# A transformer block on one core: the values of retention and attention made in one stage ahead of the heads, by seven half-size products

## The chip, the cores and the metric

The kernel runs on one core of one Trainium2 chip. The metric is the device time of one execution in microseconds (us), as the median of several runs. A core has five engines with a queue of instructions each: TensorE (PE in the profile; its weight loads are PEld), VectorE (DVE), ScalarE (ACT), GpSimd (POOL) and SyncE (SP). The instructions of one engine run in the order of its queue, and wait for others by semaphores. SyncE, ScalarE and GpSimd also issue transfers (DMAs) between the chip's DRAM and the on-chip buffers, in the same queues.

## The reference

One block works on 528 tokens (16 meta tokens and 512 real ones) of width 1024, in fp32: a feed-forward layer, a mixer, a second feed-forward layer and a last norm. The mixer has two branches that share one input projection.

```python
def hybrid_mixer(u, pos, k_top, w_in, w_ret_out, w_att_out, w_mix_out):
    proj = u @ w_in
    ...
    rq, rk, rv, rg, aq, ak, av, iq, ik, iw, g_ret, g_att = jnp.split(proj, offs, axis=-1)
    rq = rope(rq.reshape(B, T, RET_HEADS, RET_DK), pos)                      # 4 heads of 256
    rk = rope(rk.reshape(B, T, RET_HEADS, RET_DK), pos) * (RET_DK ** -0.5)
    rv = rv.reshape(B, T, RET_HEADS, RET_DV)                                 # 4 heads of 512
    yr = retention(rq.transpose(0, 2, 1, 3), rk.transpose(0, 2, 1, 3), rv.transpose(0, 2, 1, 3))
    ...
    yr = (jax.nn.silu(rg) * yr) @ w_ret_out
    aq, ak = rope(aq, pos), rope(ak, pos)                                    # 8 heads of 128
    iq, ik = rope(iq, pos), rope(ik, pos)                                    # 8 index heads of 64
    ya = dsa_attention(aq, ak, av, iq, ik, iw, k_top).reshape(B, T, ATT_W) @ w_att_out
    merged = jax.nn.sigmoid(g_ret) * yr + jax.nn.sigmoid(g_att) * ya
    return merged @ w_mix_out

def reference(...):
    h = h + 0.5 * swiglu(rmsnorm(h, ffn1_norm), ...)
    h = h + hybrid_mixer(rmsnorm(h, mix_norm), pos, k_top, ...)
    h = h + 0.5 * swiglu(rmsnorm(h, ffn2_norm), ...)
    return rmsnorm(h, final_norm)[:, N_META:]
```

The values are `rv` (2048 columns of the projection) and `av` (1024 columns). `retention` multiplies decayed query-key products by values; `dsa_attention` picks the 128 best keys of a query by the index scores and attends to them and to the meta tokens.

## The kernel before

**Products.** Activations lie transposed: width on the 128 partitions, tokens along the free axis, in eight tiles of 128 rows (`KD` = 8). An fp32 product is made of three products of parts: each operand is split into a high and a low part (`split`: ScalarE copies the high part, VectorE subtracts it for the low one), and TensorE makes high x high, low x high and high x low. `mm3` (L145) does this for a tile of 128 output columns: 8 x 3 = 24 matmuls of 128x512. Weights come from DRAM by SyncE in pieces of 512 KB or 1 MB (`load_w`, `raw`, two buffers) and are split in pieces of 128x1024 (`split_w`; `whi`, `wlo`, three buffers each). `Cols` hands out such pieces of a weight matrix, tile after tile.

**Feed-forward layers.** They use a Strassen-Winograd scheme (`Sevens`): a product in two halves on each side is made by seven half-size products in place of eight, of sums of tokens and sums of weights that VectorE makes. The steps are run by `steps_through` (L273), which interleaves by hand the split of the next weights with the matmuls of a step; there the orders of PE, ACT and DVE are written out. Elsewhere only PE's order is written out, and a scheduler orders the other engines' work.

**Mixer.** The tokens are not multiplied by their norm ahead of the projections. The factor of each token (`R`, a row over tokens copied to all partitions, or `rtok`, a column) is applied to what comes out: the rope tables are multiplied by it (`rope_tables`, L859, on GpSimd), gates are multiplied on VectorE (L1232, L1079 and `gate_a`, L1262), values are multiplied in `split_gain` (L120). The order of TensorE is:

1. Index queries (four psiq), head 0's keys (psrk), index keys (psik) and their ropes, in the pool `ixt`.
2. Four retention heads (the loop in the pool `rt`): projections of queries and keys (psrq, psrk) and the output products of the head before (`ret_out`, psro) alternate; then `values` (L1014) for this head, `decayed` (psst: key-query products and their decay, L1139), gates of the head (psrg), and the products with the values (`weigh`). Index scores (`index_steps`, pssc) and the top-k selection (`select_steps`) run in small steps in between, called by `step`.
3. Attention (the pool `ao`): keys and queries (psak, psaq) of a head, `scores`, transposes, products with values; the values of the first four heads are made ahead of head 0 (`half_values`), those of the last four in head 3. The gates of both branches stand between (`wide_gate`, `wide_gate_a`).
4. The output projections of both branches and the second feed-forward layer.

`values` makes 512 columns of values for the 512 tokens, tokens on the partitions: 96 matmuls (psv, L1037) of 128x512 on `w_in`, plus the 16 meta tokens by 32 small ones (psvl, L1049, two records each in the profile). High and low parts of the result (`vo`) stay on chip; the meta tokens' rows make a trip through DRAM (`vd`) to lie as tails under the others (`place_tails`). It is called six times: four retention heads, two halves of the attention.

Of the kernel before, what the change touches and what calls it, by code (L numbers as in the profile page):

```python
# [18 lines left out]
P = 128  # L19
# [16 lines left out]
IH = 8  # L36
# [45 lines left out]
def kernel(ctx: ExitStack, tc: tile.TileContext, x, meta, g1, wg1, wu1, wd1, gm,  # L82
# [73 lines left out]
    class Cols:  # L156
# [5 lines left out]

        def next(self):
# [34 lines left out]
    def tmp():  # L198
        return tp["pool"].tile([P, T], F32, tag="tmp", name="tmp", bufs=tp["bufs"])

    def rstd_steps(ssum, n, dim, dst, sp, psum, r=None):
# [7 lines left out]
        yield from rstd_of(col, n, dim, dst, sp, psum, P - (n - S), r)  # L209

    def rstd_of(col, n, dim, dst, sp, psum, tail, r=None):

# [4 lines left out]
        if r is None:  # L217
            r = sp.tile([P, 5], F32, tag="rcol", name="rcol", bufs=2)
# [35 lines left out]
    vd = dpool.tile([2, P, P], F32, name="vd")  # L254
# [5 lines left out]

    rtok = cpool.tile([P, 8], F32, name="rtok")
# [11 lines left out]
    def steps_through(steps):  # L273
# [8 lines left out]
        def upper(i):  # L282
            if i < len(steps):
                v = steps[i][1]()
                n, c = v.shape[1:]
                hi, lo = (wpool.tile([P, 1024 + WPAD], F32R, tag=t, name=t, bufs=3)[:, w_at[0] : w_at[0] + n * c]
# [223 lines left out]


    with pool("f1") as fp, ExitStack() as later:
# [7 lines left out]
        def mm_tile(name):  # L520
# [110 lines left out]
        with tc.manual_schedule(engines={mybir.EngineType.PE, mybir.EngineType.Activation, mybir.EngineType.DVE}):  # L631
            pss = [mm_tile("psg"), mm_tile("psg")]
# [73 lines left out]
        hidp = later.enter_context(pool("hid"))  # L706
        ttp = later.enter_context(pool("tt"))
        s1 = Sevens(T, TX, wg1, wu1)
# [12 lines left out]
        with tc.manual_schedule(engines=BUSY):  # L721
            psus = [mm_tile("psu")]
            mm3(halves(psus[0])[0], w0, xs, KD)
            psus.append(mm_tile("psu"))
            part = halves(psus[1])[0]
            mm3(part[:1], w1, xs, KD)
            psr = mm_tile("psr")
# [12 lines left out]
            pss = [mm_tile("psg")]  # L740
# [9 lines left out]
            pss.append(mm_tile("psg"))  # L750
# [7 lines left out]
            psus = [mm_tile("psu")]  # L758
# [6 lines left out]
            psus.append(mm_tile("psu"))  # L765
# [32 lines left out]
        def leave_tokens(k):  # L798

            h, l = new_x(k, XO)  # L800
            nc.gpsimd.tensor_scalar(xlast[:, k, :NM], hT[k][:, S:], gains[:, 1, k : k + 1], None, ALU.mult)
# [12 lines left out]
        steps += down(groups[-1], 6, leave_tokens)  # L814
        pipe = steps_through(steps)
        with tc.manual_schedule(engines=BUSY):
# [13 lines left out]
            s1.banks = later.enter_context(pool("f1banks", 8, PSUM))  # L830
# [19 lines left out]
        wss.close()  # L850
        sqp.append(later.enter_context(pool("sq", 1, side="right")))
        for _ in pipe:
            pass
    R = R2
    Rr = R[:, REAL]
# [3 lines left out]
    def rope_tables(i, mp):  # L859
# [4 lines left out]
        nc.gpsimd.tensor_tensor(c, c, R, ALU.mult)  # L864
        nc.gpsimd.tensor_tensor(s, s, R, ALU.mult)
        return c, s

    mixps = ExitStack()
    mmp = mixps.enter_context(pool("mxmm", 2, PSUM))
    smp = mixps.enter_context(pool("mxsm", 4, PSUM))  # L870

    def sm_tile(name):
        return smp.tile([P, S], F32, tag="sm", name=name)

    def mm_tile(name):
        return mmp.tile([P, 1024], F32, tag="mm", name=name)
# [40 lines left out]
    with pool("ixt") as ixt:  # L917
        tp.update(pool=ixt, bufs=8)
        norm = rstd_steps(ssum2, T, D, R2, ixt, lambda: mm_tile("psn"), rtok)
        pss = []  # L920
        cols = Cols(w_in, OFF_IQ, 4)
        for i in range(4):
            w = cols.next()
            ps = sm_tile("psiq")[:, :NL]
            mm3([(ps, LATE)], w, xs, KD)
            pss.append(ps)
            if i < 3:
                next(norm)
        nc.gpsimd.tensor_tensor(xlast[:, :, :NM], xlast[:, :, :NM], R[:, S:].unsqueeze(1).to_broadcast([P, KD, NM]), ALU.mult)
        cos, sin = rope_tables(0, ixt)  # L930
# [153 lines left out]
    with pool("rt") as rt:  # L1084
# [98 lines left out]
        for h in range(RH + 1):  # L1183
# [21 lines left out]
            if last_weigh:  # L1205
                last_weigh()
# [448 lines left out]
```

## Time and profile before

| | us |
|---|---|
| median of 3 runs | 1544.77 (1544.67 to 1544.82) |
| the profiled execution | 1544.25 |
| its span in the profile | 1542.3 |
| TensorE busy | 1530.0 (99%) |
| VectorE busy | 1029.2 (67%) |
| ScalarE busy | 698.5 (45%) |
| GpSimd busy | 180.0 (12%) |
| mean granted clock of TensorE | 0.998 |

The span is the time from the first to the last recorded instruction; the execution's own time is 1.95 us longer. Busy time is the time in which an engine works on at least one instruction. The mixer lies at about 360 to 1160 us. Rows of the trace are read so: in a group, source line, engine, operation, output and inputs by the program's names with their shapes, number, then busy time and mean duration in ns of one, then the idle time just before them and what ended it. In the chain and the timeline a row begins with start and duration in us.

### The profile page before, as it was taken

The numbers are of one execution on the slowest core, as the hardware profiler recorded it, in microseconds if no ns is written. First come the engines' busy times: TensorE is split into PE (matmuls) and PEld (weight loads), VectorE is DVE, ScalarE is ACT, GpSimd is POOL, SyncE is SP. The second block draws the span as 40 slices with busy tenths as digits, with TensorE's granted clock in tenths as the row PEclk, the third lists the DMA queues.
The fourth block names the chain that finished last, engine by engine and source line by source line (L and its number), as shares of the span: only waits on it lengthen the run. The fifth ranks groups of instructions, "written<-read, shape, count | busy, mean of one in ns | idle before, by whom it ended". The sixth has DMA issues, their size and how long they took to land.

```text
span 1542.3 us, 24014 instructions
## 1 busy us (share of the span) xinstructions
PE 1530.0 (99%) x9851; PEld 1380.8 (90%) x9851; DVE 1029.2 (67%) x1608; ACT 698.5 (45%) x1126; POOL 180.0 (12%) x182
## 2 busy tenths in 40 slices
PE   9999999999999999999999999999999999999998
PEld 8999999999878888788888889898888899899996
DVE  4987585775665876957445566565455788586675
ACT  6655363555543232233243465465235356254453
POOL 0000000004411101303305111110002000000000
PEclk9999999999999999999999999999999999999999
DMA  4232333235231231231413221322343223323232
GB/s 166 62 126 90 107 103 108 92 104 192 93 105 48 83 126 42 82 126 38 147 34 118 79 78 55 102 69 69 109 142 104 84 81 110 109 90 130 83 110 95
DMA packets 146862, 150.11 MB, mean 97 GB/s; under 512 B 4152, under 2 KB 129104, under 8 KB 146752
## 3 DMA queue, kind: packets, MB, share of 16 engines
q1 hardware_dynamic: 141184, 138.16, 27.7%
q10 hardware_dynamic: 4544, 9.03, 1.7%
q8 instruction: 77, 1.26, 0.3%
q0 software_dynamic: 1024, 1.39, 0.3%
q14 instruction: 33, 0.27, 0.1%
HBM read 143.59 MB, written 4.98 MB: 96 GB/s over the span
## 4 chain that ended last, share of the span: by engine, by line
PE 95%; DVE 2%; ACT 1%; issue 0%; POOL 0%; ACTq 0%; POOLq 0%
PE psqX L153 13%; PE psv L1037 8%; PE psd L153 8%; PE psd L1509 7%; PE psqY L153 7%; PE psrg L153 6%; PE psro L153 4%; PE psqZ L153 3%; PE psrk L153 3%; PE psak L153 3%; PE psu L153 3%; PE psgate L153 3%; PE psmo L153 3%; PE psaq L153 3%; PE psga L153 3%; PE psat L153 3%
## 5 line engine op out<-in xcount | busy, mean ns | idle before, releaser
L117 ACT ACTIVATE whi<-raw 128x1024 fp32r<-128x1024 f32 (+1 forms) x160 | 154.4, 968 | 317.2 <-issue 46.7
L118 DVE TENSOR_TENSOR wlo<-raw,whi 128x1024 fp32r<-128x1024 f32 (+1 forms) x160 | 194.3, 1216 | 94.5 <-ACT whi L117 94.3
L268 ACT ACTIVATE whi<-raw 128x1024 fp32r<-128x1024 f32 (+2 forms) x124 | 106.6, 862 | 96.1 <-PE psd L153 44.9
L269 DVE TENSOR_TENSOR wlo<-raw,whi 128x1024 fp32r<-128x1024 f32 (+2 forms) x124 | 121.1, 982 | 19.0 <-ACT whi L268 18.7
L153 PE MATMUL psqX<-tl,whi 128*128 128x264 f32 (+1 forms) x432 | 122.3, 283 | 0.0
L153 PE MATMUL psqX<-th,whi 128*128 128x264 f32 (+1 forms) x432 | 122.3, 283 | 0.0
L153 PE MATMUL psqX<-th,wlo 128*128 128x264 f32 (+1 forms) x432 | 122.2, 283 | 0.0
L268 ACT ACTIVATE whi<-wsum 128x1024 fp32r<-128x1024 f32 x72 | 76.3, 1060 | 70.7 <-PE psd L1509 22.0
L269 DVE TENSOR_TENSOR wlo<-wsum,whi 128x1024 fp32r<-128x1024 f32 x72 | 87.9, 1222 | 12.4 <-ACT whi L268 12.3
L153 PEld LDWEIGHTS psqX<-th,whi 128*128 128x128 f32 x432 | 82.1, 190 | 0.1
L153 PEld LDWEIGHTS psqX<-th,wlo 128*128 128x128 f32 x432 | 82.0, 190 | 0.0
L153 PEld LDWEIGHTS psqX<-tl,whi 128*128 128x128 f32 x432 | 82.0, 190 | 0.0
L153 PE MATMUL psro<-vo,whi 128*128 128x512 f32 x256 | 79.0, 390 | 0.0
L1037 PE MATMUL psv<-whi,xh 128*128 128x512 f32 x192 | 76.0, 396 | 0.0
L1037 PE MATMUL psv<-wlo,xh 128*128 128x512 f32 x192 | 74.9, 390 | 0.6 <-DVE wlo L118 0.6
L1037 PE MATMUL psv<-whi,xl 128*128 128x512 f32 x192 | 74.8, 390 | 0.0
L153 PE MATMUL psd<-hl,whi 128*128 128x264 f32 x352 | 71.4, 284 | 0.0
L153 PE MATMUL psd<-hh,wlo 128*128 128x264 f32 x352 | 70.8, 283 | 0.0
L153 PE MATMUL psd<-hh,whi 128*128 128x264 f32 x352 | 70.6, 282 | 0.0
L1509 PE MATMUL psd<-whi,hh 128*128 128x512 f32 x176 | 68.5, 389 | 0.0
L1509 PE MATMUL psd<-wlo,hh 128*128 128x512 f32 x176 | 68.5, 389 | 0.0
L1509 PE MATMUL psd<-whi,hl 128*128 128x512 f32 x176 | 68.5, 389 | 0.0
(380 smaller groups left out, 4414.0 us busy)
## 6 DMA issues: line engine op xcount, KB each, us to landing
raw<-in_w_in_dram SPq DMA_DIRECT2D x55, 512.0 KB, 3.6
raw<-in_ffn_w_up_dram SPq DMA_DIRECT2D x22, 1024.0 KB, 5.0
raw<-in_ffn_w_gate_dram SPq DMA_DIRECT2D x21, 1024.0 KB, 5.0
raw<-in_w_in_dram SPq DMA_DIRECT2D x19, 1024.0 KB, 5.2
raw<-in_ffn_w_down_dram SPq DMA_DIRECT2D x24, 512.0 KB, 3.4
raw<-in_ffn_w_down_dram SPq DMA_DIRECT2D x12, 768.0 KB, 4.3
raw<-in_w_ret_out_dram SPq DMA_DIRECT2D x16, 512.0 KB, 3.4
raw<-in_w_att_out_dram SPq DMA_DIRECT2D x4, 1024.0 KB, 4.5
```

Source lines behind the costliest of these rows:

```text
L117: nc.scalar.activation(hi, src, AF.Copy)
L118: eng.tensor_tensor(lo, src, hi.bitcast(F32), ALU.subtract)
L153: nc.tensor.matmul(o, a[:, k, :], b[:, sl], start=first and k == 0 and i == 0, stop=last and k == nk - 1 and i == 2, skip_group_check=onto)
L268: nc.scalar.activation(hi, src, AF.Copy)
L269: return lambda: nc.vector.tensor_tensor(lo, src, hi.bitcast(F32), ALU.subtract)
L1037: nc.tensor.matmul(ps[b], a[:, bs], m[:, k, :], start=k0 + k == 0 and i == 0, stop=k0 + k == KD - 1 and i == 2)
L1509: nc.tensor.matmul(ps, a[:, bs], m[:, j, :], start=first and i == 0, stop=last and i == 2)
```

## The change

The values of all heads are made in one stage between the first feed-forward layer and the mixer, appended to the steps of that layer, with the orders of PE, ACT and DVE written out:

- **Early steps.** Nine projections stand first: four of index queries, the index keys, and head 0's queries and keys. Their results are multiplied by the norm on VectorE (`normed_out`) and written to DRAM (`fq`, `fs`, `fk`) by GpSimd's queue.
- **Tokens with their norm.** Beside these steps VectorE multiplies the tokens by norm and gain in place (`with_norm`, eight operations on 128x528), makes sums of tokens (`add_ts`) and splits them. `Rr` goes out of the gates, the rope tables and the values.
- **Units.** Three units (`Values`: heads 0 and 1, heads 2 and 3, all of the attention) of seven products, in 14 steps of 12 matmuls. VectorE makes the sums of weights (`sums`); results are collected in four buffers `rm` and written to DRAM (`vst`) by GpSimd's queue; the meta tokens' rows go to `vd`.
- **Gates in the stage.** One gate after each unit (two of retention, one of attention), its sigmoid left in DRAM (`gd`); after the last unit also the first two psrg of head 0.
- **Head 0.** The rows of queries and keys are loaded again, roped from there (`rope_pair`), and psst follows directly after the last gate. The index ropes (`index_ropes`) are made from DRAM after `decayed` of head 0, rotated halves by transfers with swapped rows.
- **All heads.** `load_values` (one transfer of 1 MB and two splits of 128x1024) takes the place of `values`.
- **Attention.** The values of the first half are loaded at the start, of the second at head 1. Gates stand in every head; those of the attention are left in `gd` and loaded again at the output projection.

The core of the diff:

```diff
+        class Values:
+            PRODUCTS = [("11", "B11", "X"), ("12", "B21", "Z"), ("s2", "T2", "X"), ("s1", "T1", "Y"),
+                        ("21", "T3", "X"), ("12", "B22", "Y"), ("22", "T4", "X")]
...
+                    def run(w, lower):
...
+                        for t in range(2):
+                            for k in range(2):
+                                xh, xl = self.tokens(name, j + k, t)
+                                for m, (a, b) in enumerate(((xh, w[0]), (xl, w[0]), (xh, w[1]))):
+                                    nc.tensor.matmul(d[bank_][t], a, b[:, k, :], start=not onto and j + k + m == 0,
+                                                     stop=j + k == 3 and m == 2, skip_group_check=onto)
+                            if t == 0:
+                                lower()
...
+        units = [Values(0, OFF_RV), Values(1, OFF_RV + 2 * S), Values(2, OFF_AV)]
+        steps += [early_step(i) for i in range(len(early))]
+        steps += units[0].steps(units[1], meanwhile) + [gate_step(OFF_GR, 0)]
+        steps += units[1].steps(units[2], {}) + [gate_step(OFF_GR + P, 1)]
+        steps += units[2].steps(None, {}) + [rg_step(0), rg_step(1), gate_step(OFF_GA, KD)]
         pipe = steps_through(steps)
...
+        def with_norm(ks):
+            for k in ks:
+                nc.vector.scalar_tensor_tensor(hT[k], hT[k], gains[:, 1, k : k + 1], R2, ALU.mult, ALU.mult)
...
+    def index_ropes():
+        late = slice(P, S)
+        for i in (0, 2):
+            a, b = (ix.tile([P, 2, NL], F32, tag=f"iq{c}", name=f"iq{c}") for c in "ab")
+            nc.sync.dma_start(a, fq[:, i : i + 2, :NL])
+            for r in range(4):
+                o = r ^ 1
+                nc.scalar.dma_start(b[32 * r : 32 * r + 32], fq[32 * o : 32 * o + 32, i : i + 2, :NL])
...
+    def load_values(i, parts):
+        raw = wpool.tile([P, 2048], F32, tag="raw", name="raw", bufs=2).rearrange("p (c t) -> p c t", c=4)
+        nc.sync.dma_start(raw, vst[i].rearrange("p c b d -> p c (b d)"))
+        for c in (0, 2):
+            split(raw[:, c : c + 2], *(p[:, c : c + 2, :] for p in parts))
...
             if h == 0:
-                rk = rope_pair(*first_keys, cos, sin, T, "rk")
...
+                qs = [rt.tile([P, S], F32, tag="ossum", name="qs", bufs=2) for _ in range(2)]
+                ks = [tmp() for _ in range(2)]
+                for i in range(2):
+                    nc.sync.dma_start(ks[i], fk[i])
+                    nc.scalar.dma_start(qs[i], fs[:, 1 + i, :])
+                nc.scalar.dma_start(u, decay[h])
+                sgs = [gated(ps) for ps in first_rg]
+                rq = rope_pair(*qs, cos[:, REAL], sin[:, REAL], S, "rq")
+                rk = rope_pair(*ks, cos, sin, T, "rk")
...
+            place_tails(h)
+            vs = load_values(h, parts)
             o = []
+            prob = decayed(rq, rk, u)
             ssum = rt.tile([P, S], F32, tag="ossum", name="ossum", bufs=2)
-            vs = values(OFF_RV + h * DV, parts, rt, step)
-            prob = decayed(rq, rk, u)
-            cg = Cols(w_in, OFF_RG + h * DV, 4)
+            if h == 0:
+                index_ropes()
+                bg[0] = index_steps()
+                cg.next_at(2)
...
-                ins = nc.vector.tensor_tensor(sg, ps, Rr, ALU.mult)
-                nc.scalar.activation(sg, sg, AF.Silu)
...
             k, q = proj_k(), proj_q()
-            vs = half_values(0)
             for h in range(AH):
                 more = h + 1 < AH
-                scores(q, k, *(((2, 1, 0, 3),) if h == 4 else ()))
+                scores(q, k)
...
                 pt = transpose_p()
-                if h == 3:
-                    more_vs = half_values(1)
-                elif more:
-                    wide_gate()
-                else:
-                    wide_gate_a()
+                if h == 1:
+                    more_vs = load_values(5, [v[:, 4:, :] for v in vo])
+                wide_gate()
                 weigh_v(h, pt, vs[h])
```

More of the change, by code (lines that the diff above doesn't have):

```diff
@@ L849 @@
                 next(pipe)
[L850 to L855, printed above, removed]
+            wss.close()
+            sqp.append(sqs.enter_context(pool("sq", 1, side="right")))
+            for _ in pipe:
+                pass
+        dense.close()
+        tp["make"] = None
     w_at[0] = 0
@@ L1087 @@
         parts = [rt.tile([P, 4, S], F32R, tag=f"vo{i}", name="vo") for i in range(2)]
-        cos, sin = ret_tables
         gap(rt, 16)
```

519 lines of the change are left out of this document (355 added, 164 removed).

## The prediction

> **What bounds the kernel now.** I read the page first: busy times, granted clock, shares of the chain that ended last.
>
> ```profile
> PE 1530.0 (99%) x9851; PEld 1380.8 (90%) x9851; DVE 1029.2 (67%) x1608; ACT 698.5 (45%) x1126; POOL 180.0 (12%) x182
> PEclk9999999999999999999999999999999999999999
> PE 95%; DVE 2%; ACT 1%; issue 0%; POOL 0%; ACTq 0%; POOLq 0%
> ```
>
> TensorE works through 99% of the span at full clock, and the chain lies on it for 95%. So a matmul taken out pays its whole duration, and any new hole in TensorE's order costs its whole length. Then the table by stretches of 20 us over the mixer (360 to 1160 us; its sum row), and two stretches singled out: the end of retention head 0, and the first half of the attention values. The columns are length, then busy time of PE, PEld, DVE, ACT and POOL (with counts), clock, DMA share and GB/s.
>
> ```profile
> sum 800.00, PE 796.62 PEld 685.44 DVE 497.77 ACT 334.65 POOL 154.55; mean PE 19.92 PEld 17.14 DVE 12.44 ACT 8.37 POOL 3.86
> 520.00:540.00 20.00, 20.00 (x90) 16.54 (x89) 19.97 (x39) 5.09 (x6) 0.00 (x0) 1.00 0.40 132
> 848.30:870.00 21.70, 21.70 (x152) 17.80 (x152) 8.69 (x10) 7.29 (x10) 4.45 (x7) 1.00 0.25 72
> ```
>
> The mixer holds 3.4 us of holes in 800. VectorE is full at the end of a head, and the values that follow leave it over half idle: they are cover, 21.7 us of matmuls that ask little of the other engines. The chain (start, us, what) shows where that cover lies:
>
> ```profile
> 529.93 5.44 PE psro L153 x24
> 535.37 10.89 PE psv L1037 x48
> 546.26 1.88 PE psvl L1049 x64
> 548.14 11.10 PE psv L1037 x48
> 559.25 4.08 PE psst L1148 x30
> ```
>
> Per head the values stand between the last output product of the head before (psro) and the key-query products (psst). While they run, ropes, splits and loads finish.
>
> **What the change removes.** From the row above one 128x512 matmul lasts 10.89 / 48 = 0.2269 us. Before: six calls of 96 psv, 576. After: three units of seven products, 24 matmuls each, 504. The tails (psvl) stay the same work. So 72 matmuls go: 72 x 0.2269 = **-16.3 us**, certain if the code does what it says. The projections that move ahead (index queries and keys, head 0's queries and keys, two psrg, three gates) cost TensorE the same where they now stand. Also gone are VectorE's products with the norm and the six splits with gain:
>
> ```profile
> L1232 DVE TENSOR_TENSOR sg<-psrg,R 128x512 f32<-128x512 f32 x16 | 11.1, 692 | 44.1 <-PE psrg L153 44.1
> ```
>
> They lay beside TensorE, so I count nothing for them except -2 us (0 to -3.4) for the small waits in the 3.4 us of mixer holes that vanish or move.
>
> **What it adds: the entry to retention head 0.** TensorE's written order there is now two psrg, a psgate, then directly psst. Psst needs the rope of head 0's queries and keys, whose raw rows come back from DRAM. Let G be the end of that last psgate. Before, head 0 had 21.7 us of values at this place; now there is no cover. These rows price the chain:
>
> ```profile
> L1266 ACT ACTIVATE sa<-sa 128x512 f32<-128x512 f32 x8 | 5.0, 620 | 0.0
> L117 ACT ACTIVATE whi<-raw 128x1024 fp32r<-128x1024 f32 x126 | 132.9, 1059 | 250.7 <-issue 46.7 <-PE psrg L153 39.1 <-DMA raw<-in_w_in_dram 30.7
> raw<-in_w_in_dram SPq DMA_DIRECT2D x19, 1024.0 KB, 5.2
> 840.44 0.33 ACTq L862 DMA_DIRECT2D cos<-in_rope_dram  x1
> 840.80 0.46 ACTq L863 DMA_DIRECT2D sin<-in_rope_dram  x1
> cos<-in_rope_dram ACTq DMA_DIRECT2D x3, 264.0 KB, 3.1
> hc<-hd ACTq DMA_DIRECT2D x8, 256.0 KB, 2.7
> L1097 DVE TENSOR_TENSOR tmp<-psrq,cos 128x512 f32<-128x512 f32 x8 | 5.5, 684 | 7.4 <-PE psrq L153 7.4
> L1097 DVE TENSOR_TENSOR tmp<-psrk,cos 128x528 f32<-128x528 f32 x8 | 5.6, 702 | 9.8 <-PE psrk L153 9.8
> L118 DVE TENSOR_TENSOR rql<-tmp,rqh 128x512 fp32r<-128x512 f32 x8 | 6.2, 790 | 0.3 <-ACT rqh L117 0.2
> L1100 POOL TENSOR_TENSOR tmp<-tmp 128x512 f32<-128x512 f32 x8 | 10.7, 1343 | 18.4 <-DVE tmp L1097 18.4
> L1100 POOL TENSOR_TENSOR tmp<-tmp 128x528 f32<-128x528 f32 x8 | 12.3, 1554 | 31.1 <-DVE tmp L1097 31.1
> L117 ACT ACTIVATE rkh<-tmp 128x528 fp32r<-128x528 f32 x8 | 5.2, 646 | 10.0 <-POOL tmp L1100 10.0
> L118 DVE TENSOR_TENSOR wlo<-raw,whi 128x1024 fp32r<-128x1024 f32 x126 | 161.4, 1284 | 92.4 <-ACT whi L117 92.2
> ```
>
> ScalarE's queue at G holds, in order: the gate's sigmoid (0.62), the split of the next 1 MB of weights, then the loads of the index tables, of iw and of the two halves of the queries. The weight load can start only when an older buffer was split, about G-2.9; it lands at G+2.3, and the split ends at G+3.4. Only then are the loads issued, 0.33 to 0.46 us each: the first half of the queries at G+4.8, landing 2.7 to 3.1 later at G+7.6; the second waits for the cosine table's landing and lands at about G+9.9. SyncE has the keys behind the causal table, which waits until the gate just made has been written to DRAM: G+8 to 10. VectorE then makes four products of 0.69 for the queries (to about G+11.3) and four of 0.70 for the keys, with the query lows (0.79) among them: to about G+15.9. GpSimd adds at 1.34 and 1.55: its last ends at about G+17.9. ScalarE's rkh (0.65) makes G+18.5, the first matmul of psst. The splits of the values just loaded, 2 x 1.06 and 2 x 1.28, stand in the same queues. **+18.5 us**, 13 if loads are issued early and the splits hide, 22 if the loads collide.
>
> After such a hole TensorE is cold. The only row for that is the kernel's start:
>
> ```profile
> 1.46 4.07 PE L576 MATMUL psg<-idle 128*128 128x512 f32 x10 [1.46 <-DVE idle L544]
> ```
>
> Ten matmuls there took 4.07 us in place of 10 x 0.2269 = 2.27: **+1.8** (0 to 3). The Trainium skill, "TensorE: Matmul & The Clock Gate", Part 1, says the array runs at half clock until about 3.4 us of activity have passed; by that the loss would be an estimated 1.7 us after each long hole, 3.4 for this one and the attention's, instead of 1.8 and the 0.3 below. The start row agrees in size; no row here shows it in mid-kernel.
>
> **Index scores beside head 0.** Their rope was finished before the mixer's heads; now index_ropes runs in head 0, from DRAM, in two halves through one buffer. The second half's load waits for VectorE's low part of the first, and VectorE, which takes its work in order, stands at low parts that wait for loads.
>
> ```profile
> u<-in_decay_dram ACTq DMA_DIRECT2D x4, 384.0 KB, 3.1
> L977 ACT ACTIVATE tmp<-pssc 128x512 f32<-128x512 f32 x8 | 4.4, 590 | 1.8 <-PE pssc L974 1.7
> ```
>
> One load of 384 KB (3.1) that is half uncovered, 2.5 to 3 us; the third pair of scores waits for the second half's rope, about 4; relu at 0.59 each hardly paces it. **+7** (2 to 10).
>
> **Start of the first unit.** Beside its first steps VectorE norms the tokens (eight operations on 128x528, 0.70 each by the key's product above, 5.6 us), sums tokens and splits them. A step is 12 matmuls, 2.72 us, and gets up to 5.9 us of VectorE work there; some slack is stored. **+2.5** (0 to 5). Units two and three: 14 lows and 8 sums at 1.22 and five or so evacuations are 31 us of VectorE under 168 x 0.2269 = 38.1 of TensorE, so I take nothing.
>
> ```profile
> L269 DVE TENSOR_TENSOR wlo<-wsum,whi 128x1024 fp32r<-128x1024 f32 x72 | 87.9, 1222 | 12.4 <-ACT whi L268 12.3
> ```
>
> **Head 1.** The row 520 to 540 has VectorE full when head 0 ends. Before, values followed; now psst follows at once, and VectorE's order has two value lows (1.28 each), an accumulation, a step of the top-k, four psst evacuations and splits ahead of the low of the next psrg weights. **+4** (1 to 6). In heads 2 and 3 that low stands earlier, and there is no top-k: nothing.
>
> **Attention entry.** Before, psaq and psak were followed by 21.7 us of values. Now the scores follow at once, and the rope of the first query lies open:
>
> ```profile
> 880.31 5.78 PE psak L153 x48
> 880.40 0.59 ACT L884 ACTIVATE tmp<-psaq 64x512 f32<-64x512 f32 x1 [1.03 <-PE psaq L153]
> 881.75 1.29 POOL L887 TENSOR_TENSOR tmp<-tmp,sin 128x512 f32<-128x512 f32 x1 [13.16 <-ACT tmp L885]
> 883.80 0.64 ACT L117 ACTIVATE aq<-tmp 128x512 fp32r<-128x512 f32 x1 [1.25 <-DVE tmp L888]
> 884.82 0.68 DVE L118 TENSOR_TENSOR aq<-tmp,aq 128x512 fp32r<-128x512 f32 x1
> ```
>
> Here psaq ended at 880.31; the high part is ready at 884.44, the low at 885.50: 4.1 to the first score matmul and 0.6 more before the third kind, 0.3 for the clock. **+5** (3 to 7). The gates that now stand beside the heads of the attention replace the second half of the values; they cover as many matmuls as before.
>
> **Sum.** -16.3 - 2 + 18.5 + 1.8 + 7 + 2.5 + 4 + 5 = +20.5. The profiled execution took 1544.25 (span 1542.3 and 1.95 around it); the median of the runs is 0.5 above it. 1544.25 + 20.5 + 0.5 = **1565**. All low ends: -16.3 - 3.4 + 13 + 0 + 2 + 0 + 1 + 3 = -0.7; all high ends: -16.3 + 22 + 3 + 10 + 5 + 6 + 7 = +36.7.
>
> **Rivals.** *Faster (the other side): the loads come early.* One mechanism: if the split of the weights at G is not held by its load, the query loads go out at about G+1 rather than G+4.8, keys likewise, and VectorE and GpSimd, idle then, follow. The hole is 13 less what overlaps. With the other terms at their low ends (-13.7 together) the kernel is measurably faster from a hole under 13.7 - 3.1 = 10.6; at 5 it takes 1544.8 - 8.7 = 1536. For it: the transfers are small and the DMA share low (0.25). Against it: four products, two additions and the splits of both halves alone are over 9 us. Chance 0.07.
>
> *Break-even:* hole 13 and all others near their low ends, 1544 to 1549. For it: 3.4 us of holes in 800 show how well this kernel's order hides things. Against it: each low end needs its own luck. Chance 0.08.
>
> *Values bound by VectorE:* if in every unit the sums of weights (8 x 1.22 = 9.8) come ahead of the lows that TensorE waits for, three units lose up to 29 us: 1565 + 29 - 2.5 = 1591; half of it gives 1578. For it: VectorE's share there is 82%, and weight loads start only when the old quarter is split. Against it: the same scheme in the FFN (wsum rows) runs with TensorE at 99%. Chance 0.12.
>
> *The change saves nothing:* the count of psv would not fall to 504. The code leaves no room for that; under 0.01.
>
> The forecast keeps 0.72. **Numbers.** A measurement here tells 0.2% (3.1 us) from no change. Faster by more: the first rival and a little of the break-even's edge, 0.08. Within: half of the break-even, 0.04. Slower: 0.88. The range reaches from 1546, inside the break-even case, to 1582, the sum's high end and half of the third rival.
>
> **What would show it.** In the profile after: psv 504; a hole of 13 to 22 us ahead of the first psst with ACT rkh as its releaser, and matmuls of about 0.4 us behind it; waits of psX score products for index lows and loads; a wait of the first psS for aq of about 4; a wait of psrg in head 1 for wlo. Wrong would be: TensorE waiting under 10 us at the first psst, or waits of several us in the second and third unit.

## The result: 3.9% slower, and the profile after

| | before | after |
|---|---|---|
| median, us | 1544.77 (1544.67 to 1544.82, 4 runs) | 1604.80 (1602.45 to 1608.07, 4 runs) |
| ratio | | 1.039, 95% interval 1.0372 to 1.0409 |
| the profiled execution, us | 1544.25 | 1602.45 |
| its span, us | 1542.3 | 1600.7 |

The page of the kernel after: busy times, granted clock in 40 slices, shares of the chain.

```profile
PE 1533.6 (96%) x9779; PEld 1380.9 (86%) x9779; DVE 1088.7 (68%) x1652; ACT 726.6 (45%) x1145; POOL 169.9 (11%) x180
PEclk9999999999999978999899999999999999999999
PE 85%; DVE 5%; ACT 3%; issue 2%; DMA 2%; POOL 2%; ACTq 0%; POOLq 0%; DVEq 0%
```

TensorE has 72 matmuls fewer and is busy no shorter (1533.6 against 1530.0): some run at a lower clock, in the fifteenth, sixteenth and twentieth slices. Its holes grew from 12 us (1542.3 - 1530.0) to 67 (1600.7 - 1533.6). The chain leaves TensorE for 15% of the span instead of 5%.

Where the holes are, by the view of waits (what TensorE stood at, what released it; sum in us, times, longest):

```profile
PE psst L1422 <- ACT rkh L117: 22.9, 1, 22.9
PE psst L1422 <- DVE tmp L1426: 7.4, 3, 3.6
PE psst L1422 <- DVE tmp L1400: 5.3, 2, 3.2
PE psS L1612 <- ACT aq L117: 4.0, 1, 4.0
PE psS L1612 <- ACT gate L1354: 3.7, 4, 0.9
PE psS L1612 <- ACT gate L1561: 2.7, 3, 0.9
PE psrg L153 <- DVE wlo L118: 2.5, 1, 2.5
PE pssc L1285 <- DVE ikl L1267: 2.3, 1, 2.3
PE psaq L153 <- ACT whi L117: 1.5, 1, 1.5
```

Nothing of this size stands in the same view of before, whose longest wait is 1.5 us, at the kernel's start. The table below sets the two traces side by side by stages, each from the start of one group of matmuls to the start of another; work that moved from one stage to another (the values, 23.9 to 24.8 us a call, and three gates, 16.6 us together) is taken out of the stage it was in.

| stage | predicted | measured |
|---|---|---|
| values, their start included | -16.3 - 2 + 2.5 | -20.3 (146.4 to 126.1) |
| hole ahead of head 0's psst | +18.5 | +22.9 |
| cold clock in psst | +1.8 | +1.65 (4.15 to 5.8) |
| rest of head 0, with the index scores | +7 | +9.7 |
| head 1 | +4 | +5.5 (80.1 to 85.6) |
| heads 2 and 3 | 0 | +9.5 and +8.5 (80.5 to 90.0, 67.1 to 75.6) |
| attention entry: psak to the second head's scores | +5 | +14.1 (33.5 to 47.6) |
| the other attention heads | 0 | +6.0 (161.9 to 167.9) |
| all else (ahead of the mixer, end of the retention, end of the kernel) | 0 | +0.8 |
| sum | +20.5 | +58.4 |

The output projection (43.52 us in both) and the products from the mixer's last one to the end (393.69 and 393.72) did not change.

**The values.** One of the groups of psv matmuls, then the chain at the entry to head 0 (start, us, what), then its end in TensorE's timeline:

```profile
L1071 PE MATMUL psvX<-wlo,th 128*128 128x512 f32 x72 | 28.1, 390 | 0.0
```

```profile
569.40 4.82 DMA raw<-in_w_in_dram
574.33 2.81 DMA cos<-in_rope_dram
577.15 6.86 DMA qs<-fs
584.04 4.67 DVE tmp L1371 x4
592.26 2.28 POOL tmp L1374
595.26 4.35 PE psst L1422 x12
```

```profile
595.26 0.80 PE L1422 MATMUL psst<-rqh,rkh 128*128 128x512 f32 x1 [22.93 <-ACT rkh L117]
```

The fifteen groups at L1071 (three of 72, twelve of 24) are 504 matmuls, and no idle time stands in front of them. The three units take 42.2, 41.9 and 41.9 us. Then TensorE stands from 572.3 (G) to 595.26, and the chain is the one foretold: weights, cosine table, queries, products, additions, rkh. The first matmul behind the hole lasts 0.80 us where 0.39 was the mean of its form before. Two of the products in front of it are longer than the forecast's rows. In VectorE's timeline, the same form beside GpSimd's additions (584.82 to 588.14) and away from them:

```profile
585.25 1.77 DVE L1371 TENSOR_TENSOR tmp<-tmp,cos 128x528 f32<-128x528 f32 x1
589.83 0.70 DVE L1371 TENSOR_TENSOR tmp<-tmp,cos 128x528 f32<-128x528 f32 x1
```

The queries and keys are now read from SBUF; the products that priced them (L1097) read PSUM.

**End of heads 2 and 3.** Two stretches in the table by windows (length, busy PE, PEld, DVE, ACT, POOL, clock, DMA share, GB/s), then VectorE, GpSimd, ScalarE and TensorE there in the timeline:

```profile
755.00:775.00 20.00, 19.95 (x88) 16.00 (x87) 19.79 (x35) 3.70 (x6) 8.70 (x8) 1.00 0.36 117
775.00:786.00 11.00, 4.47 (x27) 3.86 (x26) 7.79 (x12) 4.77 (x6) 1.89 (x2) 0.70 0.11 32
```

```profile
756.59 0.68 DVE L1400 TENSOR_TENSOR tmp<-psro,rn 128x512 f32<-128x512 f32 x1
757.19 0.55 DVE L1302 MAX8 top<-score 128x8 f32<-128x384 f32 x1
757.65 1.54 DVE L118 TENSOR_TENSOR wlo<-raw,whi 128x512 fp32r<-128x512 f32 x1
759.19 0.54 DVE L1303 MATCH_REPLACE8 score<-top,score 128x384 f32<-128x384 f32 x1
759.65 0.67 DVE L1400 TENSOR_TENSOR tmp<-psro,rn 128x512 f32<-128x512 f32 x1
757.35 1.30 POOL L1401 TENSOR_TENSOR accr<-accr,tmp 128x512 f32<-128x512 f32 x1 [2.10 <-DVE tmp L1400]
777.48 1.06 ACT L117 ACTIVATE whi<-raw 128x1024 fp32r<-128x1024 f32 x1 [11.64 <-DMA raw<-in_w_in_dram]
778.57 1.23 DVE L118 TENSOR_TENSOR wlo<-raw,whi 128x1024 fp32r<-128x1024 f32 x1 [3.21 <-ACT whi L117]
779.71 0.68 DVE L1400 TENSOR_TENSOR tmp<-psro,rn 128x512 f32<-128x512 f32 x1
780.45 0.58 PE L1422 MATMUL psst<-rqh,rkh 128*128 128x256 f32 x1 [3.24 <-DVE tmp L1400]
```

Each output product (psro) is 12 matmuls, 2.72 us. VectorE's round to it, from one evacuation (L1400) to the next, is 759.65 - 756.59 = 3.06 us: evacuation, a step of the top-k, the low part of the next weights. So VectorE falls behind by 0.34 us for each psro. Then it stands 3.21 us for the high part of weights that came late, with evacuations queued behind, and psst waits 3.24 for the last of them. Before had the same round, in its own timeline:

```profile
622.36 0.69 DVE L1126 TENSOR_TENSOR tmp<-psro,rn 128x512 f32<-128x512 f32 x1
625.42 0.67 DVE L1126 TENSOR_TENSOR tmp<-psro,rn 128x512 f32<-128x512 f32 x1
```

That is 3.06 us again. There VectorE caught up during the 24.8 us of values that followed; after, psst follows at once. The values had also given the top-k its place: of its 48 steps in before, 19 stand beside two calls of values, and the last begins at 701.3, ahead of head 3's psro (722.6). After, the steps run from 671.6 to 931.6, seven of them beside head 3's psro (841.6 to 863.4). Ahead of head 1's psst the round is another one, in the timeline of after:

```profile
673.41 0.68 DVE L1397 TENSOR_TENSOR accr<-psro,rn 128x512 f32<-128x512 f32 x1
674.01 0.68 DVE L1302 MAX8 top<-score 128x8 f32<-128x512 f32 x1
674.61 0.67 DVE L118 TENSOR_TENSOR wlo<-raw,whi 128x512 fp32r<-128x512 f32 x1
675.86 0.68 DVE L1397 TENSOR_TENSOR accr<-psro,rn 128x512 f32<-128x512 f32 x1
```

It takes 675.86 - 673.41 = 2.45 us, less than a psro, with a top-k on longer rows. The first head's outputs are written into `accr` by VectorE itself (L1397); those of the later heads are added by GpSimd, and beside that addition the low part takes 1.54 us instead of 0.67.

**Attention entry.** From the chain of after, and ScalarE's queue in the timeline:

```profile
939.68 5.97 POOL accr L1401 x4
946.11 0.84 ACT vo L117
```

```profile
945.67 0.34 ACTq L1189 DMA_DIRECT2D sin<-in_rope_dram  x1
```

The additions of the last output products (L1401) and the products with the gates (L1358) keep GpSimd until 945.65. The load of the attention's sine table leaves when they end, and ScalarE's splits stand behind that issue.

### The profile page after: what moved, and what is told of

Its sections match the earlier page's. It is cut to its first block, busy times and chain, and to the rows that moved or that the text cites. A ratio compares the mean times of both kernels' runs of the same rounds, so it can differ in the third digit from the quotient of the medians.

```text
span 1600.7 us, 24057 instructions
## 1 busy us (share of the span) xinstructions
PE 1533.6 (96%) x9779; PEld 1380.9 (86%) x9779; DVE 1088.7 (68%) x1652; ACT 726.6 (45%) x1145; POOL 169.9 (11%) x180
## 4 chain that ended last, share of the span: by engine, by line
PE 85%; DVE 5%; ACT 3%; issue 2%; DMA 2%; POOL 2%; ACTq 0%; POOLq 0%; DVEq 0%
PE psqX L153 13%; PE psd L153 8%; PE psd L1806 7%; PE psqY L153 6%; PE psrg L153 5%; PE psvX L1071 4%; PE psqZ L153 3%; PE psrk L153 3%; PE psu L153 3%; PE psrq L153 3%; PE psmo L153 3%; PE psat L153 3%; PE psgate L153 3%; PE psak L153 3%; PE psaq L153 2%
## 5 line engine op out<-in xcount | busy, mean ns | idle before, releaser
L118 DVE TENSOR_TENSOR wlo<-raw,whi 128x1024 fp32r<-128x1024 f32 (+1 forms) x122 | 143.7, 1178 | 138.8 <-ACT whi L117 137.8
L117 ACT ACTIVATE whi<-raw 128x1024 fp32r<-128x1024 f32 (+1 forms) x122 | 114.4, 939 | 257.5 <-DMA raw<-in_w_in_dram 40.9
L278 ACT ACTIVATE whi<-raw 128x1024 fp32r<-128x1024 f32 (+2 forms) x138 | 121.4, 881 | 110.2 <-PE psd L153 37.5
L279 DVE TENSOR_TENSOR wlo<-raw,whi 128x1024 fp32r<-128x1024 f32 (+2 forms) x138 | 141.0, 1026 | 33.9 <-ACT whi L278 33.9
L252 POOL TENSOR_TENSOR ssum<-ssum,sq 128x528 f32<-128x528 f32 (+1 forms) x14 | 18.4, 1317 | 443.3 <-ACT sq L251 443.3
L153 PEld LDWEIGHTS psro<-vo,whi 128*128 128x128 f32 x256 | 48.0, 188 | 10.0
L153 PE MATMUL psrg<-xh,wlo 128*128 128x512 f32 x128 | 52.6, 411 | 2.5 <-DVE wlo L118 2.5
```

The source lines that it names most:

```text
L117: nc.scalar.activation(hi, src, AF.Copy)
L118: eng.tensor_tensor(lo, src, hi.bitcast(F32), ALU.subtract)
L153: nc.tensor.matmul(o, a[:, k, :], b[:, sl], start=first and k == 0 and i == 0, stop=last and k == nk - 1 and i == 2, skip_group_check=onto)
L252: eng.tensor_tensor(ssum[:, :n], ssum[:, :n], sq[:, :n], ALU.add)
L278: nc.scalar.activation(hi, src, AF.Copy)
L279: return lambda: nc.vector.tensor_tensor(lo, src, hi.bitcast(F32), ALU.subtract)
```

## The experiments

All edits are against the kernel after; medians are compared with its 1604.8, ratios with runs of before on the same chip (1544.4 to 1545.15; e9, e10 and e11 ran on another chip than the rest). Stages are those of the table, from one profiled execution each.

### Heads 1 to 3: late weights or a full VectorE?

My first theory for the 18 us in heads 2 and 3 was the late load: `load_values` takes one of the two `raw` buffers, so the next weights leave late. The rival was VectorE's load.

**e1_inplace**: values land in the buffer of their low part.

```diff
-        raw = wpool.tile([P, 2048], F32, tag="raw", name="raw", bufs=2).rearrange("p (c t) -> p c t", c=4)
+        hi, lo = parts
+        raw = lo.bitcast(F32)
```

> The changed kernel (median 1604.8) with one edit: load_values no longer takes one of the two raw weight buffers; the 1 MB of values lands in the low part's own buffer and is split there in place. VectorE and ScalarE do the same work. Theory (a late weight load blocks VectorE's queue): in heads 1 to 3 the load of the first psrg weights no longer waits behind the value load, the low part of those weights no longer stands unready ahead of the evacuations of psro and psst, and the stalls inside psst (7.4 + 5.3 us by the waits) and the cold clock behind them go: 15 to 22 us less over heads 1 to 3, 2 to 6 less at the two entries, so 1577 to 1588. Rival (VectorE has too much work at the end of a head now that the values no longer stretch it): the amount is the same, so under 4 us less, 1600 to 1606.

1593.76 us (ratio 1.0316, 1.0301 to 1.0332). Head 1 from psst to psro went from 63.87 to 58.68, nearly all that it had lost (5.2 of 5.5); the hole ahead of head 0 lost 2.7. Heads 2 and 3 gave 1.6 and 0.5. Waits of e1:

```profile
PE psst L1423 <- ACT rkh L117: 20.2, 1, 20.2
PE psS L1613 <- ACT aq L117: 11.2, 1, 11.2
PE psst L1423 <- DVE tmp L1427: 5.1, 2, 2.6
PE psst L1423 <- DVE tmp L1401: 4.5, 2, 2.5
```

The late load is head 1's cause, and a small part of heads 2 and 3: psst there still waits for VectorE. (The 11.2 us at the attention's entry are taken up under e6.)

**e5_topk**: the steps of the top-k stand behind the gates of the head (psrg) instead of the output products.

```diff
-                step(ins)
+                if ret_steps:
+                    step(ins)
...
-                step()
+                for _ in range(4 if h else 1):
+                    step(ins if h else None)
```

> The changed kernel (1604.8) with one edit: the steps of the top-k selection (MAX8 and MATCH_REPLACE8, 1.2 us of VectorE together) no longer stand behind each psro evacuation, but four of them behind each psrg of heads 1 to 3. The same work elsewhere. Theory now (two causes at the end of a head: a late weight load that stops VectorE, and VectorE over-full with 3.05 us of work for each psro of 2.72): the second goes, the first stays: 4 to 10 us less in heads 2 and 3, 1595 to 1601. Rival (only the late load): under 2 us less, 1603 to 1606.

1590.51 us (1.0295, 1.0278 to 1.0311), 14.3 less. psst to psro in head 2 fell from 67.78 to 59.89, in head 3 from 53.84 to 47.09; before had 58.28 and 45.37. Head 1, ahead of whose psst VectorE's round fits under a psro, kept 63.91. The value load still takes a `raw` buffer, so the theory of the late load fell for heads 2 and 3: it is VectorE's backlog, which frees the `raw` buffers late as well. In head 2 the load of the first psrg weights leaves 15.2 us after the first psro, in after 19.8. (Head 0 became 3.4 us longer and its hole 2.0; why, no run shows. The hole was 22.9 to 25.1 in after, e2, e4 and e6, whose edits do not touch it.)

### Head 0: the entry

**e3_rgfirst**: the other two psrg of head 0 ahead of psst.

```diff
+            if h == 0:
+                cg.next_at(2)
+                more_rg = []
+                for _ in range(2):
+                    ...
+                    mm3([(ps, REAL)], w, xs, KD)
```

> The changed kernel with one edit: the third and fourth psrg of head 0 (48 matmuls, 10.9 us) stand ahead of the first psst instead of behind it. Theory (the hole of 22.9 us ahead of psst is lost cover): the hole shrinks to about 12 us and 6 to 11 us of the time go, less what the index scores lose of their cover: 1594 to 1601. Rival (head 0 is set by the chain of loads and ropes as a whole, index ropes included): the time comes back as waits of the index scores and of the first products with values, under 3 us gained, 1602 to 1606.

1595.97 us (1.0333, 1.0317 to 1.0348). Waits of e3:

```profile
PE psst L1422 <- ACT rkh L117: 12.2, 1, 12.2
PE pssc L1285 <- ACT ikh L1266: 4.9, 1, 4.9
```

The hole shrank by the 10.9 us put into it. But from psst to psro head 0 took 66.56 instead of 70.70 - 10.9 = 59.8: the index scores, that much nearer to psst now, wait for their ropes. A good part came back at the next late thing.

**e7_early**: head 0's loads go out on SyncE, in order of need (tables, keys and queries first, index and causal tables last).

```diff
-    cos, sin = rope_tables(2, rtab)
+    nc.sync.dma_start(cos, rope[2, 0])
+    nc.sync.dma_start(sin, rope[2, 1])
...
+                    nc.sync.dma_start(qs[i], fs[:, 1 + i, :])
...
+                nc.sync.dma_start(caus, causal)
```

> The changed kernel with one edit: the loads of head 0's entry (rope tables, queries, keys, decay, index tables, causal table) go through SyncE's queue in the order in which they are needed, none through ScalarE's. Theory (ScalarE's queue stands at the split of a weight load that lands 2 us after the last gate, and the loads behind it): the ropes start about 6 us earlier, the hole of 22.9 us becomes 15 to 18: 5 to 8 us less, 1597 to 1600. Rival (ropes on VectorE and GpSimd set the entry): under 3 us, 1602 to 1605.

1593.48 us (1.0318, 1.0302 to 1.0335). The hole is 17.1 instead of 22.9: the late issue on ScalarE's queue was some 6 us of it. Of the rest 4.7 us pass until the first product of the ropes (577.11), and 12.4 are the work of the ropes with the splits among it. The wait of pssc for ikh is 6.3.

**e9_gates**: the three gates of the value stage moved to head 0, one ahead of psst and two behind it.

```diff
-        steps += units[0].steps(units[1], meanwhile) + [gate_step(OFF_GR, 0)]
+        steps += units[0].steps(units[1], meanwhile)
...
+            if h == 0:
+                left_gate(Cols(w_in, OFF_GA, 1), KD)
...
+                left_gate(g_cols, 0)
+                left_gate(g_cols, 1)
```

> The changed kernel (1604.8) with one edit: the three gates made inside the value stage (24 matmuls, 5.5 us each) are made in head 0 instead, one ahead of psst and two behind it. The same matmuls in another place. Theory (the value stage needs no cover and head 0 has none): the value stage shortens by 16.5 us, the hole ahead of psst shrinks by 5 to 8 and the holes around the index scores by 5 to 9: 10 to 16 us less, 1589 to 1595. Rival (head 0 is set by the amount of VectorE work, the gates add splits to it): under 4 us less, 1601 to 1606.

1586.32 us (1.0274, 1.0259 to 1.0288), 18.5 less, the most of any one edit. The hole is 8.2 instead of 22.9, with one gate (5.5 us) standing in it: the other 9.2 go because the loads are no longer queued behind the stage's last gate. The two halves of the queries leave 6.1 and 1.6 us ahead of the end of the stage's last matmul; in after they leave 3.3 and 4.8 us behind it. From psst to psro head 0 grew by 13.2, of which the two gates are 11.

**e10_fill**: 95 matmuls on data at hand, their result unused, in the hole.

> The changed kernel with one addition: 95 idle matmuls of 128x512 (21.5 us at full clock) between the last psgate and the first psst of head 0, whose results nothing reads; they fit into the hole of 22.9 us. Theory (the hole lets the granted clock fall, and psst behind it runs at about half for 1.6 us more than before): psst of head 0 takes 4.2 us again in place of 5.8, the clock stays at 1.00 up to it, the total 1 to 2 us less or within the spread: 1602 to 1605. Rival (psst is slow for another reason, its operands or PSUM buffers): psst stays at 5.8 us and the total does not fall.

1597.39 us (1.0339, 1.0324 to 1.0353). Windows of e10, one over the hole and one behind it; its first psst matmul; then the windows of after:

```profile
572.00:596.00 24.00, 21.81 (x96) 17.57 (x94) 13.53 (x13) 7.58 (x10) 10.56 (x17) 1.00 0.45 151
596.00:602.00 6.00, 4.75 (x30) 3.86 (x30) 5.63 (x8) 1.70 (x4) 0.00 (x0) 1.00 0.70 224
```

```profile
596.31 0.50 PE L1422 MATMUL psst<-rqh,rkh 128*128 128x512 f32 x1 [2.50 <-ACT rkh L117]
```

```profile
572.00:595.00 23.00, 0.34 (x2) 0.00 (x0) 13.48 (x13) 7.60 (x10) 10.47 (x17) 0.56 0.47 162
595.00:602.00 7.00, 6.74 (x34) 5.68 (x35) 5.78 (x11) 2.35 (x5) 0.00 (x0) 0.75 0.67 211
```

With TensorE kept at work the clock stays at 1.00 and the matmul takes 0.50 instead of 0.80. But psst as a whole is no shorter, 5.88 us up to psrg against 5.80: at full clock it stands for VectorE instead (0.29 us for rkl, 0.65 for an evacuation), and the expected 4.2 did not come. Head 0 from psst to psro is 67.81 instead of 70.70; these 2.9 us lie at the first index scores and the gate behind them. (The way from the last gate to psst is 1.3 longer.) The median fell by 7.4, more than that. Most of the rest (3.65 us) is at the attention entry, which the edit does not touch; psak to the first scores lay anywhere between 18.8 and 22.6 us in the profiles of kernels whose edits stand elsewhere. The gains of e5, e7 and e9 hold 3.0 to 3.5 us of the same. So this median doesn't size the clock, and the +14.1 of the table would be some 10.5 with the shortest of these.

### Attention

**e6_attin**: tables of the attention loaded in head 2, products with the two gates left in DRAM made in attention heads 4 and 5.

```diff
+            if h == 2:
+                for i, t in enumerate(att_tables):
+                    nc.sync.dma_start(t, rope[1, i])
...
-            gate_acc(c, t)
...
+                if h in (4, 5):
+                    ...
+                    gate_acc(h - 4, t)
```

> The changed kernel with one edit in two places: the rope tables of the attention are loaded in head 2 into buffers of their own, and the two gates that come back from DRAM are multiplied in behind attention heads 4 and 5, not at the end of the retention. Theory (at the attention's entry GpSimd works off 8 additions and 4 products until 8 us after psak began, and the table loads, ScalarE's queue and the rope stand behind its buffers): the entry, 22.4 us from psak to the first psS where the matmuls and one rope need 15.7, loses 4 to 7 us: 1598 to 1601. Rival (late weights of psak and psaq alone): under 2 us, 1603 to 1606.

1601.99 us (1.0372, 1.0357 to 1.0386). psak to the first scores fell from 22.41 to 17.69, below all other profiles without this edit (18.8 and more). Up to the second head's scores, though, the entry is 43.8 us, as in e10. The trace of e1 says more. Its weights come in time, psak and psaq wait for none, and still its entry up to the first scores takes 22.58 us, with 11.2 of waiting for the rope. GpSimd's additions end there at 938.27, and the chain goes on:

```profile
938.29 7.49 DMA sin<-in_rope_dram
```

The sine table's load leaves when the additions end, as in after. So GpSimd's queue and this load make a long entry without late weights; in e10 the chain runs through late weights. How much of the 14.1 each makes is not settled.

**e4_attgate**: one of the gates of the attention heads (5.5 us) ahead of the first scores.

```diff
+            wide_gate()
```

> The changed kernel with one edit: one gate of the attention branch (24 matmuls, 5.5 us) stands between the first psak/psaq and the first scores, and one less at the output projection. Theory (the rope of the first query lies open for 4.0 us, with 1.6 us of cold clock behind it): 4 to 6 us less at the entry, 0 to 2 us more at the output projection, 1599 to 1603. Rival (the late weights of psak and psaq set the entry, with them everything moves): no change, 1603 to 1607.

1599.53 us (1.0352, 1.0335 to 1.0369). The entry up to the second head's scores took 47.1 us with the gate in it, 47.6 without; the other heads fell from 167.91 to 162.34. The gate stood free in the entry, which has at least that much hole.

**e2_gcopy**: VectorE copies a gate's sums out of PSUM, and ScalarE's sigmoid works on the copy.

```diff
-        nc.scalar.activation(t, ps, AF.Sigmoid)
+        nc.vector.tensor_copy(t, ps)
+        nc.scalar.activation(t, t, AF.Sigmoid)
```

> The changed kernel with one edit: the gates of the attention stage are first copied out of PSUM by VectorE (as before, where the product with the norm did it), and ScalarE takes the sigmoid from SBUF. 11 more VectorE instructions of 0.69 us. Theory (the psS of the next head waits 0.9 us for the PSUM buffer that ScalarE's sigmoid frees late): the waits of psS for the gate go, 0.9 to 1.1 us in each of 7 heads, 5 to 8 us less, 1597 to 1600. Rival (VectorE's load decides): no gain or 2 to 8 us more, 1605 to 1613.

1595.77 us (1.033, 1.0315 to 1.0345). The seven waits for `gate` (3.7 + 2.7 us) are gone, and the attention heads from the second on take 161.36 instead of 167.91; before, the same work took 161.9. That is their whole loss.

### Together

**e8_all**: the seven edits e1 to e7.

> All seven edits so far together (values landed in place, gate copied out by VectorE, two psrg ahead of psst, a gate at the attention's entry, top-k steps behind psrg, attention tables early, loads of head 0 early). Theory (the 18 us that the seven products save are real, and everything lost behind them is cover and queue order): the losses of 77 us shrink to 12 to 25, 1539 to 1552, level with before (1544.8). Rival (the load on VectorE and GpSimd per head is too high without the values between): the edits overlap and 40 us or more remain, 1565 or more.

1555.14 us (1.0069, 1.0056 to 1.0082): 49.7 of the 60 are back, less than expected. Heads 2 and 3 are at 58.66 and 45.77, the attention heads at 156.2 with one gate outside. What is left is head 0, in the waits of e8:

```profile
PE pssc L1283 <- ACT ikh L1264: 4.6, 1, 4.6
PE psst L1427 <- ACT rkh L117: 4.3, 1, 4.3
```

**e11_best**: e8 with e9's gates, and the rope of the index keys first, in buffers of its own.

> All nine edits together: the seven of the run of all edits (1555.1), the three gates moved to head 0, and the index keys' rope as the first of the index ropes, in buffers of its own. Theory (what is left of the loss, 19 us, lies in head 0 around the index scores and is lost cover): 10 to 18 us less, 1537 to 1545, under or level with before (1544.4). Rival (VectorE's work in head 0, full from 620 to 690, sets that stage): under 5 us less, 1550 or more.

1545.19 us (1.0001, 0.9992 to 1.001): level with before. Its longest new wait:

```profile
PE psst L1427 <- ACT tmp L1545: 6.0, 1, 6.0
```

L1545 is the sigmoid of the gate ahead of psst: a PSUM buffer comes free late, since ScalarE has the index splits in front.

**e12_order**: e11 with all three gates behind psst, the index loads ahead of them on SyncE, and the index ropes held until the fifth evacuation of psst.

```diff
+                first = index_loads(rt)
+                left_gate(Cols(w_in, OFF_GA, 1), KD)
...
-                index_ropes(rt)
+                with tc.issue_after(evacs[4].ins):
+                    index_ropes(*first)
```

> The nine edits (1545.2, level with before) with two orders changed in head 0: all three gates stand behind psst instead of one ahead of it, and the index ropes are issued behind psst's evacuations, their loads ahead of them. Theory (there the queries and keys are roped in time, and psst only waits 6.0 us for a PSUM buffer that ScalarE frees behind the index keys' split, with cold clock behind it): the wait goes, 5 to 9 us less, 1536 to 1541, under before (1544.7). Rival (the index ropes then come later and their scores wait instead): under 2 us less, 1543 to 1547.

1540.46 us (1539.76 to 1541.81, 8 runs), ratio 0.9971 (0.9961 to 0.9982): 4.7 us faster than before, so the change can pay when its cover is rebuilt. The page of e12:

```profile
PE 1517.2 (99%) x9779; PEld 1371.9 (89%) x9779; DVE 1092.9 (71%) x1663; ACT 727.8 (47%) x1145; POOL 178.6 (12%) x180
```

TensorE's busy time is now 12.8 us below that of before. By stages, against before: values -20.3, head 0 +6.0, head 1 +2.2, head 3 +0.4, attention entry +5.8, all else +1.7. Whether some of these edits would also have helped before was not run; its holes were 12 us in all.

## Why the prediction failed in size

The direction, the mechanism (cover lost) and the largest single hole were right; the size was not: +60 against +20, and above the sum of all high ends (+36.7). Step by step:

- **Values removed.** Right: 504 matmuls, 20.3 us saved where 16.3 + 2 were counted. The +2.5 for the first unit's start did not come: no unit has a hole, so the rival of values bound by VectorE did not happen either.
- **Entry to head 0.** Right in its chain, 4.4 us short in size, and just above the upper bound of 22. The weights landed at G + 1.9 (forecast 2.3), but the load of the queries took 6.86 us behind its issue (577.15) instead of 2.7 to 3.1 and landed at G + 11.7 (forecast 9.9); from there to psst it took 11.2 instead of 8.6. The products were priced at 0.70 by rows that read PSUM; two of them took 1.77 and 1.76, with inputs from SBUF beside GpSimd's additions. e7 shows that the issue order was about 6 us of the hole. The forecast's bounds assumed one thing going wrong at a time.
- **Cold clock.** +1.65 against 1.8. The granted clock over psst was 0.75 (1.00 in e10), and its first matmuls start 0.43 us apart (597.31 and 597.74 in the timeline of after) instead of 0.23. The Trainium skill ("TensorE: Matmul & The Clock Gate", Part 1) states half clock after an idle window; this spacing agrees. But e10 shows that VectorE would have held psst at full clock too. Two things were not counted: behind the 2.3 us wait of pssc for ikl the clock was 0.50 from 612.4 to 622.0, and the holes in heads 2 and 3, 3.2 and 3.0 us in one head, lowered it too (0.70 in 775 to 786).
- **Index scores.** +9.7 against +7, inside the bounds, with 2.3 us of waiting for the index keys' low part (ikl); e3 and e7 show the wait for `ikh` at 4.9 and 6.3 when psst comes earlier.
- **Head 1.** +5.5 against +4. psrg waits 2.5 us for wlo, which stands behind value lows and evacuations in VectorE's order, as named; e1 shows what the forecast did not name: the weights' load left late.
- **Heads 2 and 3: the step that failed.** The forecast gave "nothing", because the weights' low part stands earlier there and there is "no top-k". That is wrong twice. The top-k is there: the steps that stood beside the values now fall into later heads, until the last one. (In before six of them stood beside the psro ahead of head 2 already; "no top-k" held for head 3 alone.) And beside these heads VectorE's round is longer, not shorter, than ahead of head 1, 3.06 us against 2.45. The row 520 to 540 of the prediction, with VectorE at 19.97 of 20, had shown a head that ends with VectorE full; I used it for head 1 alone. The backlog, 0.34 us for each psro, with the cold clock and the waits behind it, costs 18 us where the values no longer hide it; e5 takes 14.6 of them away, and with late weights gone too (e8) nothing of it is left in head 2 and 0.4 in head 3.
- **Attention entry: the term that was mis-sized.** +14.1 (10.5 to 14 with the spread) against +5. I priced the rope (the wait of psS for aq is 4.0, as foretold) and left out what stands in front of it: GpSimd's additions and gate products until 945.65, and the table loads and late weight splits behind them. Before, 24.5 us of values covered this. The trace of e1 shows the additions and the table load with 11.2 us of waiting behind them.
- **Attention heads: a second step that failed.** "They cover as many matmuls as before" is true of TensorE's time, but the gate's PSUM buffer is now freed by a sigmoid in ScalarE's queue instead of a product on VectorE. That is 0.9 us, seven times (e2). The products on VectorE that I counted as free to remove had a use: they freed PSUM early.

Three failed or mis-sized terms, 18 + 9.1 + 6 = 33 us, make nearly all of the 38 us between forecast and result; the entry's 4.4, head 0's 2.7, head 1's 1.5 and 0.8 elsewhere less the values' 4.5 are the rest.

## What to carry to other kernels

When a block of matmuls is taken from between the stages of a loop, it is cover that is taken: list for every iteration, and every place where it stood, what each other engine still has to do at that moment, backlog included, and price it, not only the first iteration. Ask also where the work goes that was issued beside the block: here 19 of the 48 top-k steps moved into stages that had no room for them. A row that shows an engine at 99% in one iteration is a reason to read the same row of the others. When an instruction is dropped from an idle engine, ask which buffer it freed, and who frees it now.

## What the runs showed of the hardware

The low part of 128x512 weights takes VectorE 0.67 us alone (the row at 674.61) and more than twice that beside a GpSimd operation on SBUF: the one at 757.65 began during GpSimd's addition of 757.35 to 758.65, took 1.54 us and ended 0.54 after that addition. An operation that reads PSUM is not held up. This evacuation began inside GpSimd's addition of 772.59 to 773.89:

```profile
773.55 0.68 DVE L1400 TENSOR_TENSOR tmp<-psro,rn 128x512 f32<-128x512 f32 x1
```

The other side can wait as well. In e5 a low part began at 769.34 and took 0.68 us; GpSimd's addition, begun at 769.50, took 1.67 instead of 1.29.

The Trainium skill, "SBUF — State Buffer", section "SBUF: two separate sides", says that an operation of VectorE with two SBUF inputs and one of GpSimd that reads SBUF exclude each other for a whole instruction. The rows agree. Here this is the difference between a round of 2.45 us that fits under a psro of 2.72 and one of 3.06 that does not: an addition on an engine that is 11% busy fills another one. The gain of e5 holds both, the top-k's 1.2 us and the 0.87 that the low parts no longer wait in most of its rounds; the two were not separated. A version with these additions elsewhere was not run.
